# A longer ring for the expert weights, lent from the end's sum

## The chip, the cores and the metric

The kernel runs on one core of a Trainium2 chip. The metric is the time of one execution on the device, in microseconds (us); for the kernel before it is the median of three runs. One more execution was recorded by the hardware profiler, and all rows below are from it.

## The reference

One layer of a conditioned hybrid decoder: 1024 tokens of width 1024 (T and D below), all float32. Shift, scale and gate vectors come from a projection of a conditioning vector.

```
h   = modulate(x)                          # shift and scale of the conditioning vector
x1  = LayerNorm(alpha*x + gate * mixer(h)) # conformer convolution beside an SSD scan, one output projection
h2  = modulate(x1)
MoE : top group of 8, then the top 2 of its 8 experts (64 experts in all)
      y = (silu(h2 @ w1[e]) * (h2 @ w3[e])) @ w2[e],  w1, w3: 1024x512, w2: 512x1024
      f = sum over the token's 2 experts of gate_prob * y
out = LayerNorm(alpha*x1 + gate2 * f)      # ln2_g, ln2_b
```

Each expert has 3 matrices of 2 MB. All 64 experts are 384 MB, and the kernel reads nearly all of it once.

## The kernel before

The program has three stages, one after the other. The first (to about 940 us) computes the adaLN projection, the input projection, the convolutions, the scan and the output projection; its last step is the output projection `mix` (L480), for which SP loads the weights `wo` (L927). It ends with a router for each 128 tokens, and it leaves the normalised rows x1 without their scale and shift in DRAM, in `td`. The second (to about 955 us) builds tables: which token stands in which place of which expert, as one-hot comparisons `rows` (L1214 to L1221) that are multiplied on TensorE, with the index columns `gidx` and `ridx` as the result. The third is the mixture of experts, and then the second LayerNorm, here called the end.

The third stage does 32 units, in a fixed order by a string of letters (ORDER). A unit gathers 128 rows of `td` by `gidx` (L1294, POOL), transposes them (`tp`, L1302), and multiplies: h0 and h1 (L1332) with w1 and w3, a product and a transpose (`s1`, `hT`, L1337 to L1344), and yp (L1351) with w2. VectorE scales the result to y (L1356), and POOL scatters it to `ybuf` by `ridx` (L1288). A unit is made of one expert with 128 rows (H), two experts with 64 (F and L) or four with 32 (S); a T is a pair of experts with three units, `t`, `t..x` and `t`, where the middle one uses both. So S takes 24 weight tiles of 1 MB, L and F take 12, H takes 6, and T takes 12 for three units. In names such as `h0t4x` or `yps` the letters after h0, h1 or yp are the kind of unit. The last unit is an S; 18 of its 24 tiles are loaded only on a condition, that an expert has rows, which does not hold for these inputs.

The weight tiles (`load`, L238 to L243, [128, 2048] float32) come on SP's queue in the order of use. `plan` numbers all 384 of them, and the ring has N_RING = 14 slots: tile n goes to `ring[n % 14]`, and is asked for when the last use of tile n - 14 has been emitted. Slots 0 to 7 (N_RING_A) belong to a pool that lives through the first stage; four of them (4 to 7) carry the `wo` columns before. 13 tiles (N_EARLY) are asked for before the first gather: 4 in the program step F ahead of `wo_2_5` and the later ones, and so on through `load_fixed`, whose expert numbers are known before the tables.

The end's sum needs acc = alpha*(ln1_g*td + ln1_b) for each 128 tokens. `load_sum(i)` (L1270 to L1278) does row block i: a load on ScalarE's queue (L1275), a multiply and an add on VectorE (L1276, L1277), a scaling on ScalarE (L1278). It is called after the units 4 to 11, one for each. The first call loads ln1_g and ln1_b too, into a tile with the tag yb (L1274).

The end (`finish`, L1541 to L1586) does eight row blocks. `collect` (L1280 to L1285) loads, on POOL's queue, both experts' y of each token from `ybuf`: block 0 into the tile `yb`, the other blocks into ring slots that have come free. A block's z is acc plus these two plus the last unit's own y, which is not sent through DRAM but is added by one-hot matrices (`hots` times `yhs` and `yls`, L1366 to L1373). VectorE adds one part to acc (L1556), TensorE sums the rest into PSUM (L1549 to L1560), VectorE takes the statistics (L1561, L1563), and VectorE, ScalarE and POOL normalise (L1565 to L1585). SP stores the rows (L1586). Each queue and engine works through its instructions in the order in which they were emitted; the compiler's scheduler sets that order.

The loads of the tiles wait for slots on SP's queue. Loads issued by SP and ScalarE share eight completion counters (lanes), and a new load waits until the last one of its lane has landed.

## Time and profile before

| what | value |
|---|---|
| median of three runs | 2002.7 us (2000.44 to 2003.66) |
| profiled execution: time | 2007.87 us |
| profiled execution: span, first to last instruction | 2006.1 us |
| mean granted TensorE clock | 0.959 of full speed |
| busy: PE, PEld, DVE, ACT, POOL | 89%, 50%, 48%, 28%, 25% of the span |
| bytes moved on SP's and ScalarE's queues | 551.74 MB and 42.34 MB |

PE is TensorE's matmuls, PEld its weight loads, DVE VectorE, ACT ScalarE, POOL GpSimd, SP the engine that issues most transfers. The profiled execution took 5.2 us more than the median of the runs. Busy shares are means over the three stages, which have different limits; the third stage, from about 955 us on, is to be read by itself.

### The profile page before, as it was taken

Reading aid. Unit: us, or ns where it says so; the run is one execution under the profiler, and the core shown is the slowest. Engines: PE = TensorE matmul, PEld = TensorE weight load, DVE = VectorE, ACT = ScalarE, POOL = GpSimd, SP = SyncE. Lnnn points to the kernel's source line nnn. Section 1 sums busy time; section 2 is a strip of 40 time slices with the busy share of each in tenths; the row PEclk is TensorE's granted clock in tenths of the full one; section 3 lists DMA queues with packets and bytes.
Section 4 is the critical chain, followed back from the end, with each engine's and each line's share of the span. In section 5 each row is a group of like instructions: output and inputs, shape, how many; then the busy total and the mean of one; then the engine's idle time right before and its main releaser. Section 6 shows DMA issues by size and latency. Waiting matters only on the chain.

```text
span 2006.1 us, 23809 instructions
## 1 busy us (share of the span) xinstructions
PE 1789.1 (89%) x8136; PEld 998.1 (50%) x8136; DVE 956.2 (48%) x1928; ACT 557.4 (28%) x1054; POOL 501.6 (25%) x408
## 2 busy tenths in 40 slices
PE   6899999899999999997879799788898997999786
PEld 1566667587788777886323133232242331443233
DVE  1699999869998997867113012112011110111117
ACT  0345554643555465644100011011010010111001
POOL 0457656513443465311100001000000000000014
PEclk7899999889999999998889899999999998999998
DMA  7788888656655446674899999999989999999993
GB/s 242 234 293 265 260 254 300 223 195 212 203 190 192 160 150 221 218 289 163 316 419 419 420 415 354 419 419 420 420 300 391 419 420 419 418 412 371 419 366 161
DMA packets 202328, 620.81 MB, mean 309 GB/s; under 512 B 25886, under 2 KB 91702, under 8 KB 154332
## 3 DMA queue, kind: packets, MB, share of 16 engines
q1 hardware_dynamic: 155792, 551.74, 71.8%
q10 hardware_dynamic: 36188, 42.34, 6.6%
q0 software_dynamic: 10224, 25.18, 3.3%
q8 instruction: 65, 1.06, 0.2%
q14 instruction: 59, 0.48, 0.1%
HBM read 575.07 MB, written 79.25 MB: 326 GB/s over the span
## 4 chain that ended last, share of the span: by engine, by line
PE 45%; DMA 31%; DVE 11%; issue 5%; ACT 4%; POOL 3%; ACTq 0%; SPq 0%; DVEq 0%; POOLq 0%
DMA ring<-in_expert_w_dram 25%; PE mix L480 6%; PE px L480 5%; PE h0h L1332 3%; DVE ac L605 2%; PE pg L480 2%; PE h1h L1332 2%; PE pv L480 2%; PE pz L480 2%; PE yph L1351 2%; PE yps L1351 2%; PE ypl L1351 2%; PE h1l L1332 2%; PE h0l L1332 2%; PE ypt L1351 1%
## 5 line engine op out<-in xcount | busy, mean ns | idle before, releaser
L605 DVE SCALAR_TENSOR_TENSOR ac<-u,cw,ac 128x512 f32<-128x512 f32 x394 | 295.7, 750 | 5.5
L1294 POOL DMA_INDIRECT xg<-td,gidx x32 | 32.9, 1027 | 754.8 <-PE tph L1302 206.7
L480 PE MATMUL px<-hTh,wx_hl 128*128 128x512 f32 x512 | 169.8, 401 | 1.6 <-DVE u L619 1.2
L1332 PE MATMUL h1s<-ring,xTs 128*32 128x512 f32 x512 | 105.2, 733 | 43.2 <-DMA ring<-in_expert_w_dram 43.2
L480 PE MATMUL mix<-wo_hl,cth 128*128 128x512 f32 x416 | 129.9, 405 | 1.7 <-ACT zs L726 1.1
L1351 PE MATMUL yps<-ring,hTs 128*32 128x512 f32 x512 | 109.1, 613 | 19.3 <-DMA ring<-in_expert_w_dram 16.8
L1338 DVE TENSOR_TENSOR s1s<-s1s,h1s 128x512 f32<-128x512 f32 x8 | 5.5, 688 | 220.8 <-PE h1s L1332 220.8
L480 PEld LDWEIGHTS px<-hTh,wx_hl 128*128 128x128 f32 x512 | 95.6, 188 | 30.4 <-issue 4.6
L454 POOL TENSOR_TENSOR wo_hl<-wo,wo_hl 128x512 fp32r<-128x512 f32 x52 | 74.0, 1436 | 113.3 <-ACT wo_hl L453 106.1
L480 PE MATMUL px<-hTl,wx_hl 128*128 128x512 f32 x256 | 101.3, 396 | 0.0
L480 PE MATMUL pg<-hTh,wg_hl 128*128 128x512 f32 x256 | 89.2, 419 | 2.0 <-DVE h L520 1.8
L480 PEld LDWEIGHTS mix<-wo_hl,cth 128*128 128x128 f32 x416 | 78.2, 190 | 22.0 <-DVE wo_hl L454 1.5
L1332 PE MATMUL h0s<-ring,xTs 128*32 128x512 f32 x512 | 75.4, 639 | 14.0 <-DMA ring<-in_expert_w_dram 14.0
L311 PE MATMUL ada<-wada,cond 128*32 128x512 f32 x192 | 67.7, 706 | 19.7 <-DMA wada<-in_w_ada_dram 19.7
L480 PE MATMUL pv<-hTh,wv_hl 128*128 128x512 f32 x256 | 84.0, 396 | 0.0
L480 PE MATMUL pz<-hTh,wz_hl 128*128 128x512 f32 x256 | 83.6, 397 | 0.1
L1332 PEld LDWEIGHTS h1s<-ring,xTs 128*32 128x32 f32 x512 | 22.6, 129 | 121.0 <-DMA ring<-in_expert_w_dram 76.6
L480 PE MATMUL mix<-wo_hl,ctl 128*128 128x512 f32 x208 | 77.6, 404 | 3.1 <-DVE ctl L962 3.1
L453 ACT CAST wo_hl<-wo 128x512 fp32r<-128x512 f32 x104 | 62.9, 617 | 33.0 <-PE mix L480 18.1
L1351 PEld LDWEIGHTS yps<-ring,hTs 128*32 128x32 f32 x512 | 26.7, 111 | 87.4 <-issue 46.4
L1351 PE MATMUL ypl<-ring,hTl 128*64 128x512 f32 x256 | 66.6, 598 | 2.3 <-ACT hTl L1344 2.3
L1332 PE MATMUL h0l<-ring,xTl 128*64 128x512 f32 x256 | 63.6, 598 | 3.9 <-DMA ring<-in_expert_w_dram 3.9
(622 smaller groups left out, 3465.5 us busy)
## 6 DMA issues: line engine op xcount, KB each, us to landing
ring<-in_expert_w_dram SPq DMA_DIRECT2D x384, 1024.0 KB
wo<-in_w_out_dram SPq DMA_DIRECT2D x112, 256.0 KB
wada<-in_w_ada_dram SPq DMA_DIRECT2D x96, 256.0 KB
wind<-wx_hl SPq DMA_DIRECT2D x32, 512.0 KB
wx_hl<-wind SPq DMA_DIRECT2D x32, 512.0 KB
wind<-wg_hl SPq DMA_DIRECT2D x16, 512.0 KB
wind<-wv_hl SPq DMA_DIRECT2D x16, 512.0 KB
wx<-in_w_in_dram SPq DMA_DIRECT2D x32, 256.0 KB
```

The costliest lines, as they stand in the source:

```text
L311: nc.tensor.matmul(pm[32 * j:32 * j + 32, :], lhs, wt, start=(k == 0), stop=(k == KT - 1), tile_position=(0, 32 * j))
L453: nc.scalar.copy(hi, wt)
L454: (eng or nc.gpsimd).tensor_tensor(lo, wt, hi, op=OP.subtract)
L480: nc.tensor.matmul(pt, lhs[a_], rhs[b_], start=(first and n == 0), stop=(last and n == 2))
L605: nc.vector.scalar_tensor_tensor(to, v_, w_, run_, op0=OP.mult, op1=OP.add)
L1294: nc.gpsimd.indirect_dma_start(out=t_, out_offset=None, in_=td, in_offset=bass.IndirectOffsetOnAxis(ap=gcol, axis=0), bounds_check=T - 1, ...
L1332: nc.tensor.matmul(hp[a:b, :], xT[:, 4 * hf + k, a:b], w_[:, k, :], start=(hf + k == 0), stop=(hf + k == 4), tile_position=(0, a))
L1338: nc.vector.tensor_tensor(s1, s1, hps[1], op=OP.mult)
L1351: nc.tensor.matmul(yps[n][a:b, :], hT[:, 2 * hf + k, a:b], w_[:, k, 512 * n:512 * n + 512], start=(hf + k == 0), stop=(hf + k == 2), tile_ ...
```

## The change

The ring gets 20 slots. Ten belong to the pool that lives from the first stage on, four to the second pool, and six are lent: a new tile `lent`, the four quarters of `acc`, and one tile `lend`. Up to tile 339 all 20 slots are used in turn; for the last 44 tiles (N_BACK) only the 14 own ones, by the lists `slot` and `before`. 16 tiles are asked for ahead of the first gather.

As acc now holds weights, `load_sum` is called for all eight blocks after the unit with index len(units) - 3, the first of the last two L units. ln1_g and ln1_b are loaded into `lent`, which later takes block 0 of `ybuf`. The one-hot table `rows` has a tile of its own, and the last unit's hots and its y's high half lie in the tile with the tag `lend`.

```diff
@@ -30,9 +30,11 @@
 EPS = 1e-5
 BIG = 1.0e30
 OOB = float(1 << 20)
-N_RING = 14
-N_RING_A = 8
-N_EARLY = 13
+N_RING = 20
+N_RING_A = 10
+N_EARLY = 16
+N_LEND = 6
+N_BACK = 44
@@ -1146,6 +1148,7 @@
     toff = rt2.tile([P, 8], F32, name="toff")
     nc.gpsimd.iota(toff, pattern=[[P, 8]], base=0, channel_multiplier=0, allow_small_or_imprecise_dtypes=True)
     acc = rt2.tile([P, 8, D], F32, name="acc")
+    lent = rt2.tile([P, 2048], F32, name="lent")
     gidx = rt2.tile([P, NU_STAT], I32, name="gidx")
     ridx = rt2.tile([P, NU_STAT], I32, name="ridx")
     ridx_o = rt2.tile([P, NU_OVF], I32, name="ridx_o")
@@ -1176,7 +1179,8 @@
         def t2(nm, shape, dt=F32):
             return wk.tile(shape, dt, name=nm)
         V = nc.vector
-        ring += [ringb.tile([P, 2048], F32, name=f"ring{j}") for j in range(N_RING_A, N_RING)]
+        ring += [ringb.tile([P, 2048], F32, name=f"ring{j}") for j in range(N_RING_A, N_RING - N_LEND)]
+        ring += [lent] + [acc[:, 2 * j:2 * j + 2, :].rearrange("p a d -> p (a d)") for j in range(4)] + [None]
         load_fixed(ring, N_RING_A, N_EARLY, fix_i)
@@ -1211,7 +1215,7 @@
         V.scalar_tensor_tensor(u_, over, 4096.0, u_, op0=OP.mult, op1=OP.add)
         V.tensor_tensor(r_, r_, pos, op=OP.add)
         b16 = lambda t_: t_[:, :, None].to_broadcast([P, 16, NU_STAT])
-        rows = acc[:, 0, :].bitcast(BF16).rearrange("p (j t) -> p j t", t=P)
+        rows = t2("rows", [P, 16, P], BF16)
         hot = t2("hot", [P, 16, NU_STAT], BF16)
         V.tensor_tensor(hot, jf[:, None, 0:NU_STAT].to_broadcast([P, 16, NU_STAT]), b16(u_), op=OP.is_equal)
         hv = t2("hv", [P, 2, 16, NU_STAT], BF16)
@@ -1260,6 +1264,7 @@
         bufs_of = {"z": ZPB, "h0": 1, "h1": 1, "tp": TPB, "yp": 2}
         g2_bc = wk.tile([P, D], F32, bufs=1, name="g2_bc")
+        ring[N_RING - 1] = wk.tile([P, 2048], F32, tag="lend", bufs=1, name="lend")
         uno = [0]
         half = [slice(512 * n, 512 * n + 512) for n in range(2)]
@@ -1268,8 +1273,7 @@
         def load_sum(i):
             if i == 0:
-                l1_ = wk.tile([P, 2, D], F32, tag="yb", bufs=1, name="l1")
-                l1[:] = [l1_[:, 0], l1_[:, 1]]
+                l1[:] = [lent[:, 0:D], lent[:, D:2 * D]]
                 for t_, v_ in zip(l1, (ln1_g, ln1_b)):
                     tc.keep_in_program_order(nc.scalar.dma_start(t_, bc(v_, 0, D)))
             tc.keep_in_program_order(nc.scalar.dma_start(acc[:, i, :], td[i * P:(i + 1) * P, :]))
@@ -1280,7 +1284,7 @@
         def collect():
             for i in range(8):
-                yy = wk.tile([P, 2, D], F32, tag="yb", bufs=1, name="yb") if i == 0 else spare[i].rearrange("p (k d) -> p k d", k=2)
+                yy = (spare[i] if i else lent).rearrange("p (k d) -> p k d", k=2)
                 nc.gpsimd.dma_start(yy, ybuf[2 * i * P:2 * (i + 1) * P, :].rearrange("(t k) d -> t k d", k=2))
                 yield yy
@@ -1362,13 +1366,15 @@
             nc.vector.tensor_scalar(trel, toff, -1.0, tcol, op0=OP.mult, op1=OP.add)
             hots = []
             for j in range(0, 8, HW):
-                hot = wk.tile([P, HW, P], F32R, tag="hot", bufs=1, name=f"hot{nm}_{j}")
+                held = wk.tile([P, 2048], F32R, tag="lend", bufs=1, name="held")
+                hot = held[:, 0:HW * P].rearrange("p (j t) -> p j t", t=P)
                 nc.vector.tensor_tensor(hot, jf[:, None, :].to_broadcast([P, HW, P]),
                                         trel[:, j:j + HW, None].to_broadcast([P, HW, P]), op=OP.is_equal)
                 hots += [hot[:, i, :] for i in range(HW)]
             ys = []
+            yls = wk.tile([P, D], F32R, tag="xT", bufs=BF[0], name=f"yl{nm}")
             for n in range(2):
-                yh, yl = (wk.tile([P, 512], F32R, tag=f"y{p_}", bufs=2, name=f"y{p_}{nm}_{n}") for p_ in "hl")
+                yh, yl = held[:, D + 512 * n:D + 512 * n + 512], yls[:, half[n]]
                 nc.scalar.copy(yh, y[:, half[n]])
                 nc.vector.tensor_tensor(yl, y[:, half[n]], yh, op=OP.subtract)
                 ys.append((yh, yl))
@@ -1472,11 +1478,11 @@
             while sent[0] < len(plan):
                 n = sent[0]
-                if n >= N_RING and uses[n - N_RING] > 0:
+                if before[n] is not None and uses[before[n]] > 0:
                     break
                 r, which, hf = plan[n]
                 if n >= min(N_RING, 6 * N_FIX):
-                    load(ring[n % N_RING], *place_regs(r), which, hf)
+                    load(ring[slot[n]], *place_regs(r), which, hf)
                 sent[0] += 1
         def need(rs, times):
@@ -1493,7 +1499,7 @@
                 n = where[r, which, hf]
                 assert n < sent[0]
                 uses[n] -= 1
-                return ring[n % N_RING]
+                return ring[slot[n]]
             return of
         units = []
@@ -1525,16 +1531,26 @@
             add(kind, first[kind])
             first[kind] += step[kind]
         assert list(first.values()) == [P_TRI, P_HVY, P_LGT, P_SML, NE]
+        slot, before = [], []
+        turn = [(s_, None) for s_ in range(N_RING)]
+        for n in range(len(plan)):
+            while n >= len(plan) - N_BACK and turn[0][0] >= N_RING - N_LEND:
+                turn.pop(0)
+            s_, b_ = turn.pop(0)
+            slot.append(s_)
+            before.append(b_)
+            turn.append((s_, n))
         emitted()
         for n, (nm, places, u) in enumerate(units[:-1]):
             if n == 3:
                 overflow_tables()
             unit(nm, [tiles(r) for r in places], cols_of(u))
-            if 4 <= n < 12:
-                load_sum(n - 4)
-
-
-        spare = [ring[(len(plan) + j) % N_RING] for j in range(N_RING)]
+            if n == len(units) - 3:
+                for i in range(8):
+                    load_sum(i)
+
+
+        spare = [ring[s_] for s_, _ in turn]
         l2g_bc, l2b_bc = spare[0][:, 0:D], spare[0][:, D:2 * D]
         banks = [("z", "z"), ("h0", "h1"), ("tp", "tp"), ("yp", "yp")] * 2
```

The compiled order of the instructions shows what moves. Line numbers of the changed kernel are four to sixteen higher.

ScalarE in the kernel before, from its last product `s1s` to the end's first operations; the eight loads of acc stand far ahead of this, between the units 4 and 12:

```order
L1344 COPY hTl_12411<-thl_12406 128x512
L1309 ACTIVATE xTs_12444<-tps_0_12445,modc 128x128 x4
L1337 ACTIVATE s1s_12539<-h0s_12463 128x512
L1590 DMA ring_8112<-in_ln_g_dram 128x1024
L1591 DMA ring_8112<-in_ln_b_dram 128x1024
L1344 COPY hTs_12547<-ths_12542 128x512
L1372 CAST yhs_0_12590<-ys_12583 128x512
L1372 CAST yhs_1_12594<-ys_12583 128x512
L1565 ACT_TABLE_LOAD
```

ScalarE now, from the last unit's `s1s` to the load of the fifth row block (acc<-td is the load of a row block, acc<-acc the scaling of the one before, held the high half of the last unit's y):

```order
L1341 ACTIVATE s1s_12547<-h0s_12471 128x512
L1282 ACTIVATE acc<-acc 128x1024
L1279 DMA acc<-td 128x1024
L1606 DMA ring_6721<-in_ln_g_dram 128x1024
L1607 DMA ring_6721<-in_ln_b_dram 128x1024
L1348 COPY hTs_12555<-ths_12550 128x512
L1282 ACTIVATE acc<-acc 128x1024
L1279 DMA acc<-td 128x1024
L1378 CAST held<-ys_12591 128x512 x2
L1282 ACTIVATE acc<-acc 128x1024
L1279 DMA acc<-td 128x1024
```

These are the loads of the third, fourth and fifth row block. Ahead of these rows the load of the first stands behind the hT of unit 29, with two loads into lent before it, and the load of the second behind the last unit's `xT` copies. Behind these rows the pair of a scaling and a load comes three times more, then the last scaling and the ACT_TABLE_LOAD. So each load stands behind the scaling of the row block before, and four of the eight are behind the casts of the last unit's y.

VectorE in the kernel before, from the last unit's y (ys) on (BN_STATS are the statistics of the second LayerNorm, the adds with yb and ring those of the rows from `ybuf`):

```order
L1356 SCALAR_TENSOR_TENSOR ys_12583<-yps_0_12549,gslot,g_bc 128x512
L1556 TENSOR_TENSOR acc<-acc,yb 128x1024
L1373 TENSOR_TENSOR yls_0_12591<-ys_12583,yhs_0_12590 128x512
L1356 SCALAR_TENSOR_TENSOR ys_12583<-yps_1_12550,gslot,g_bc 128x512
L1556 TENSOR_TENSOR acc<-acc,ring_8133 128x1024
L1373 TENSOR_TENSOR yls_1_12595<-ys_12583,yhs_1_12594 128x512
L1561 BN_STATS bs_12621<-z_0_12609 128x6
L1556 TENSOR_TENSOR acc<-acc,ring_8648 128x1024
L1561 BN_STATS bs_12644<-z_0_12613 128x6
L1556 TENSOR_TENSOR acc<-acc,ring_8649 128x1024
```

VectorE now, from the seventh block's add of its rows from `ybuf` on (L1280 and L1281 are the multiply and the add of the eighth block with ln1_g and ln1_b, in lent):

```order
L1572 TENSOR_TENSOR acc<-acc,ring_8116 128x1024
L1280 TENSOR_TENSOR acc<-acc,lent 128x1024
L1281 TENSOR_TENSOR acc<-acc,lent 128x1024
L1572 TENSOR_TENSOR acc<-acc,ring_8137 128x1024
L1572 TENSOR_TENSOR acc<-acc,lent 128x1024
L1577 BN_STATS bs_12625<-z_0_12613 128x6
L1577 BN_STATS bs_12648<-z_0_12617 128x6
L1577 BN_STATS bs_12648<-z_1_12618 128x6
L1577 BN_STATS bs_12671<-z_0_12621 128x6
L1577 BN_STATS bs_12671<-z_1_12622 128x6
```

The statistics, which stood between the adds, now stand behind the last of the eight adds, and that last one is the add of block 0 from lent. The transfers that feed the adds are POOL's:

```order
L1288 DMA ring_6722<-ybuf 128x2048
L1288 DMA ring_6723<-ybuf 128x2048
L1288 DMA ring_6724<-ybuf 128x2048
L1288 DMA ring_8074<-ybuf 128x2048
L1288 DMA ring_8095<-ybuf 128x2048
L1288 DMA ring_8116<-ybuf 128x2048
L1288 DMA ring_8137<-ybuf 128x2048
L1288 DMA lent<-ybuf 128x2048
L1600 TENSOR_TENSOR lent<-lent,ring_6721 128x512
```

The load of block 0 into lent was the first of eight and is now the last; it takes the place of ln1_g and ln1_b, so it is behind the last operation of VectorE that reads them.

## Rows read from the trace of the kernel before

**Rows 1.** The view of busy time by stretches of 20 us over the third stage. The columns are the stretch in us, its length, the busy us of PE, PEld, DVE, ACT and POOL with the number of instructions, the granted TensorE clock as a share of full speed, the mean busy share of the DMA engines, and what they moved in GB/s.
```profile
940.00:960.00 20.00, 9.26 (x73) 8.12 (x73) 13.69 (x57) 2.28 (x4) 2.26 (x2) 0.50 0.14 41
960.00:980.00 20.00, 18.88 (x82) 6.78 (x82) 2.06 (x5) 5.17 (x11) 0.99 (x1) 0.89 0.71 270
980.00:1000.00 20.00, 20.00 (x96) 7.55 (x92) 2.78 (x6) 0.81 (x2) 2.02 (x2) 1.00 1.02 418
...
1180.00:1200.00 20.00, 19.15 (x85) 8.56 (x83) 4.51 (x8) 1.76 (x4) 2.03 (x2) 1.00 1.01 413
1200.00:1220.00 20.00, 19.71 (x66) 8.10 (x66) 6.27 (x10) 2.91 (x6) 2.96 (x2) 1.00 0.82 313
1220.00:1240.00 20.00, 18.86 (x72) 7.91 (x72) 5.82 (x9) 3.54 (x7) 3.07 (x2) 1.00 0.94 363
...
1460.00:1480.00 20.00, 18.86 (x91) 8.11 (x92) 2.62 (x6) 2.59 (x6) 2.04 (x2) 1.00 0.85 317
1480.00:1500.00 20.00, 19.15 (x62) 8.46 (x58) 3.46 (x7) 0.87 (x2) 2.04 (x2) 1.00 0.66 224
1500.00:1520.00 20.00, 19.71 (x79) 7.69 (x80) 2.78 (x6) 2.32 (x6) 2.03 (x2) 1.00 0.95 353
1520.00:1540.00 20.00, 18.60 (x122) 6.32 (x118) 3.46 (x7) 2.59 (x6) 2.03 (x2) 1.00 1.01 412
...
1800.00:1820.00 20.00, 18.86 (x55) 8.99 (x54) 3.37 (x7) 1.60 (x4) 2.04 (x2) 1.00 0.94 367
1820.00:1840.00 20.00, 19.66 (x120) 6.49 (x118) 2.87 (x6) 1.59 (x4) 2.03 (x2) 1.00 0.88 337
...
1980.00:2000.00 20.00, 10.87 (x30) 5.32 (x29) 15.21 (x29) 4.29 (x8) 14.06 (x10) 0.88 0.42 172
```

**Rows 2.** The chain that ended last, in order of time, around one of the pairs that make three units (start us, us, what); the chain is the piece of work, or of a transfer, that the next one waited for.
```profile
1144.49 26.09 DMA ring<-in_expert_w_dram
...
1176.65 7.13 PE ypt L1351 x16
...
1200.49 7.09 PE ypt4x L1351 x32
```

**Rows 3.** The waits of SP's queue from 850 us on (what was waited for: us in total, times, longest).
```profile
SPq L243 <- DMA ring<-in_expert_w_dram: 503.5, 254, 11.5
...
SPq L243 <- PE h0t L1332: 22.6, 5, 8.0
...
SPq L243 <- PE h0t6x L1332: 17.0, 2, 13.2
```

**Rows 4.** SP's timeline around the early weight tiles (start us, us, queue, line, operation, out<-in, count).
```profile
869.95 16.01 SPq L243 DMA_DIRECT2D ring<-in_expert_w_dram  x8
891.08 21.24 SPq L927 DMA_DIRECT2D wo<-in_w_out_dram  x14
```

**Rows 5.** VectorE's timeline in the routing step (start us, us, engine, line, operation, out<-in, shape), two of its small operations.
```profile
941.60 0.16 DVE L1237 TENSOR_TENSOR rest<-gate_all,gp 128x16 f32<-128x16 f32 x1
...
945.07 0.42 DVE L900 TENSOR_REDUCE pos_all<-r_po 128x4 f32<-128x256 f32 x1
```

**Rows 6.** ScalarE's timeline at the start of the loads for the end's sum (columns as in rows 5).
```profile
1153.16 0.34 ACTq L1274 DMA_DIRECT2D l<-in_ln_g_dram  x1
1155.65 0.34 ACTq L1274 DMA_DIRECT2D l<-in_ln_b_dram  x1
```

**Rows 7.** The view of one tile, td, the matrix of token rows in DRAM: its direct loads into acc (duration of the issue in ns, minimum, median and maximum, and the first and last start in us), and the time to landing of the transfers that name it.
```profile
L1275 ACTq DMA_DIRECT2D acc<-td x8: 326/327/353, 1158.8 to 1351.7; - x8
...
DMA to landing us min/median/max: 3.7/8.4/10.0
```

**Rows 8.** The view by lines, from 960 to 1950 us: the three operations on a loaded row of acc (busy us, mean ns | idle before, releaser).
```profile
L1277 DVE TENSOR_TENSOR acc<-acc,l 128x1024 f32<-128x1024 f32 x8 | 9.8, 1223 | 0.2
L1276 DVE TENSOR_TENSOR acc<-acc,l 128x1024 f32<-128x1024 f32 x8 | 9.7, 1218 | 1.5 <-DMA acc<-td 1.5
...
L1278 ACT ACTIVATE acc<-acc 128x1024 f32<-128x1024 f32 x8 | 8.4, 1054 | 29.8 <-DVE acc L1277 19.4 <-DMA ring<-in_expert_w_dram 10.4
```

**Rows 9.** The DMA issues from 1930 us to the end (KB each, median us from issue to landing).
```profile
ring<-ybuf POOLq DMA_DIRECT2D x7, 1024.0 KB, 11.6
...
yb<-ybuf POOLq DMA_DIRECT2D x1, 1024.0 KB, 7.7
```

**Rows 10.** VectorE's timeline at the end of the program (columns as in rows 5).
```profile
1955.00 0.75 DVE L1356 SCALAR_TENSOR_TENSOR ys<-yps,gslot,g_bc 128x512 f32<-128x512 f32 x1 [9.53 <-PE yps L1351]
...
1959.80 0.69 DVE L1561 BATCH_NORM_STATS2 bs<-z 128x6 f32<-128x512 f32 x1
...
1993.76 1.77 DVE L1582 SCALAR_TENSOR_TENSOR ring<-ring,rs,ring 128x1024 f32<-128x1024 f32 x1
```

**Rows 11.** The view by lines of VectorE from 1955 to 1996 us: the adds of the sum.
```profile
L1556 DVE TENSOR_TENSOR acc<-acc,ring 128x1024 f32<-128x1024 f32 x7 | 9.3, 1330 | 0.0
```

**Rows 12.** TensorE's timeline in one of the last rows of the sum (columns as in rows 5).
```profile
1982.00 1.02 PE L1549 MATMUL z<-ring,ident 128*128 128x512 f32 x2
1982.46 0.79 PE L1559 MATMUL z<-yhs,hots 128*128 128x512 f32 x1
1983.09 0.40 PE L1559 MATMUL z<-yls,hots 128*128 128x512 f32 x1
1983.32 1.02 PE L1560 MATMUL z<-acc,ident 128*128 128x512 f32 x2
```

## Prediction

> **What bounds the kernel now.** I read the stretches of the third stage first. The reader is to look at the GB/s column [rows 1]: in most stretches the transfers move 418 to 420 GB/s, at a busy share of 1.0 (the stretch from 980 to 1000) [rows 1], so a tile of 1 MB (1.0486 million bytes) costs 2.50 us, and the stage is bound by the weight stream. What can be won there is the time in which the stream stands: the start (940 to 980), two places around the T units (1180 to 1240, 1460 to 1540), and 1800 to 1840. The chain [rows 2] shows the same: it is a weight transfer up to 1170 us and TensorE's own matmuls in the T units that follow. The waits of SP's queue tell which release is late there. Most of the queue's waiting, 503.5 us, is for the stream itself; but a wait for a matmul such as h0t (22.6 us) or h0t6x (17.0 us) is one for a slot [rows 3]. A T needs 12 tiles, thus 30 us of stream, while its three units keep TensorE busy for 72 us (three times some 24 us, the distance from one ypt to ypt4x in the chain). The ring fills, and the stream stops.
>
> Then I read the end. It starts with the last unit's y, which VectorE takes at 1955.0, and VectorE's last operation is done at 1995.5 [rows 10]: 40.5 us in which VectorE hardly rests. The rest up to the span's end, 10.6 us, I leave as it is.
>
> **What the change gives, before the last unit's y.** Losses are against 419 GB/s: 20 us times the missing share.
>
> *Start.* Two stretches lose 18.0 us (41 GB/s) and 7.1 us (270 GB/s) [rows 1]. Three tiles more ahead of the gather use 7.5 us of the first, and four tiles behind it, where one was, fill the 7.1 us of the second. That is 14.6 us. Against it: the order puts some eight small VectorE operations of 0.16 us behind the reduction that gives pos_all [rows 5], on the path to the gather's index, 1.2 us. And SP now asks for ten tiles, not eight, ahead of the next `wo` columns, 5.0 us more stream. Between the eighth tile and the next `wo` load SP now stands from 885.96 to 891.08 [rows 4], 5.1 us, so the two fit in the gap; I charge 2 us of the possible 5 to the projection. Start: 14.6 - 1.2 - 2 = about 11 us (8 to 13).
>
> *First pair place, 1180 to 1240* (413, 313 and 363 GB/s): 0.3 + 5.1 + 2.7 = 8.0 us [rows 1]. Six slots more are 15 us of stream ahead, which covers it: 8 us (5 to 8).
>
> *Second, 1460 to 1540* (317, 224, 353, 412): 4.9 + 9.3 + 3.2 + 0.3 = 17.7 us [rows 1]. The six slots cover 15 of it: 15 us (9 to 17.7).
>
> *1800 to 1840* (367 and 337): 2.5 + 3.9 = 6.4 us [rows 1], covered: 6.4 us (3 to 6.4). The last 44 tiles have 14 slots again, as before.
>
> *Moved bytes.* The eight loads of acc, 0.5 MB each, leave the stretch 1158.8 to 1351.7 [rows 7], and ln1's 1 MB goes with them: 12.5 us of stream. About a third of that stretch is the first pair place, where they cost nothing, so 8.4 us go; ln1 and perhaps three rows come back ahead of the last y, partly where the stream is about to end. I take 4 us (0 to 8.4).
>
> *ScalarE's queue near the end.* Three loads now stand there ahead of the transposes' copies of the next unit. When such loads were issued before, they came at 1153.16 and 1155.65 [rows 6], one tile's time apart: each waited for a weight tile in its lane. I charge 2 us (0 to 5).
>
> Together 11 + 8 + 15 + 6.4 + 4 - 2 = **42.4 us** earlier at the last y (bounds, term by term, 20 to 54; the low ends all together are unlikely).
>
> **What it costs, behind the last y.** Let Y be the start of VectorE's first operation on that y. The order shows four loads of acc behind the casts of y, each behind the scaling of the row block before it. So the cover that hid them, units 4 to 11, is gone, and each link of the chain is a load, a multiply, an add and a scaling. A load's own landing was not shown; the transfers naming td, gathers of the same 512 KB, took 3.7 us at the least and 8.4 us in the median, under the full stream [rows 7]. Once the weights have ended the load is nearest to the least, so I take 3.7. With 1.22, 1.22 and 1.05 us [rows 8] and 0.4 us for hand-overs a link is 7.6 us. The fifth row's load is issued at about Y + 5, behind the two casts and the fourth row's scaling. The eighth row's add is done at Y + 5 + 3 x 7.6 + 3.7 + 2.4 + 0.4 = Y + 34.3. The Trainium skill, page "DMA: Bandwidth & Descriptors", section "Anatomy of one DMA", gives 2.0 us plus the bytes at 436 GB/s, an estimated 3.2 us for such a load; by it the chain would be 2 us shorter. No row here shows a load that short.
>
> Only then may block 0 of `ybuf` be loaded into lent. Its like took 7.7 us alone and 11.6 us beside others [rows 9]; I take the first, as nothing else moves: Y + 42. The add of 1.3 us [rows 11] ends at Y + 43.3. All statistics now stand behind that add. Before, 1959.8 to 1995.5, 35.7 us, held six of the adds, 8.0 us [rows 10, 11], so 27.7 us of VectorE are left: the end is at Y + 71.0, not Y + 40.5. That is **30.5 us** later (bounds: 24.4 with a link of 7.0 and a reload of 4.0; 49 with every load at 8.4). Moving the hots comparison and the new places of the y halves cost nothing: they lie in units in which VectorE waits for TensorE.
>
> **Sum.** -42.4 + 30.5 = -11.9 us. Against the profiled execution that is 2007.9 - 11.9 = 1996.0. It lies 5.2 us above the median of the runs, a difference that is in no term, so against the median I forecast 2002.7 - 11.9 = **1990.8 us**, faster.
>
> **Rivals.**
>
> *A: more is won.* All stalls go and the tail's chain is short: 13 + 8 + 17.7 + 6.4 + 8.4 = 53.5 us won, 24.4 lost: 1973.6. For it: the stream is at its rate wherever slots are free. Against it: the last pair place is longer than six slots, and ScalarE's loads wait in lanes. Chance 0.17.
>
> *B: TensorE's clock.* In the chain of loads TensorE has next to nothing to do, and its granted clock was 0.50, the level of 1.2 GHz, in the routing step where it was busy for 9.3 of 20 us, and 0.88 in the last rows of the end [rows 1]. A row block's z takes 1.02 + 0.79 + 0.40 + 1.02 = 3.2 us of TensorE there [rows 12], about VectorE's own pace. At half the clock four blocks take 4 x 3.2 = 12.8 us more, and the sum is +0.9: 2003.6, no change. Against it: the clock came back within 20 us at the stage's start, to 0.89 and 1.00 [rows 1]. The Trainium skill, page "TensorE: Matmul & The Clock Gate", section "What's actually happening", says that an idle array falls to half its clock and that activity brings it back; by that rule this rival's first rows of z would be slow and the later ones not. The trace agrees with the fall. Chance 0.13.
>
> *C: slower, by the chain of loads alone.* The seven loads of `ybuf` rows, 1 MB each, are under way around Y too. If each of the four loads takes 8.4 us, not 3.7, the tail loses 4 x 4.7 = 18.8 us more, and the time is 2002.7 - 11.9 + 18.8 = 2009.6. It decides from a load of 3.7 + 11.9/4 = 6.7 us on. For it: the median of rows 7. Against it: `ybuf` is some 17 us of transfers, and the chain is longer. Chance 0.13.
>
> *D: the ring does not fill.* If it is TensorE's order of releases and not the number of slots that stops the stream, the three stalls stay: 11 + 4 - 2 = 13 us won, 30.5 lost, 2020.2. Against it are the waits for h0t and h0t6x, which are waits for slots [rows 3]. Chance 0.07.
>
> **How the numbers follow.** My forecast has 0.50. A measurement of this kernel tells 0.2% (4 us) from no change. Faster: 0.50 + 0.17 = 0.67; the same: B, 0.13; slower: C and D, 0.20. The range from 1974 to 2009 reaches from A's figure to C's and leaves out D and about half of what A and C have beyond their figures. Cases of one sign hold most of the chance; the forecast's own range is 1984 to 1997.
>
> **What would show it.** In the changed profile the stretches around the T units hold 400 GB/s or more, and SP's waits for h0t and h0t6x shrink; the stream starts about 11 us earlier; the last y is at about 1955.0 - 42 = 1913. Behind it VectorE idles for DMA acc<-td four times, 3 to 5 us each; the first statistics come about 43 us after y, and the last operation some 71 us after it. I am wrong if the last y is not at least 32 us earlier, if statistics come less than 35 us behind it, or if TensorE is what VectorE waits for in the last four row blocks.

## The result and the profile after

The changed kernel takes 2022.2 us (median of five runs, 2013.9 to 2022.5) against 2002.7 us: the ratio is 1.009, with a 95% interval of 1.0069 to 1.011. It is slower, by some 18 us by the ratio (19.5 us between the medians); forecast was 1990.8 us and faster. The profiled execution has a span of 2020.4 us, 14.3 us more than before, and it splits in two at the last unit's y. That y starts at 1930.1 us, not 1955.0: 24.9 us won, where 42.4 were forecast. From there to VectorE's last operation it takes 78.1 us, not 40.5: 37.6 us lost, where 30.5 were forecast. Behind that operation the rest is 12.1 us, not 10.6.

The stretches of the third stage that answer to [rows 1], with the same columns:

```profile
940.00:960.00 20.00, 9.04 (x71) 7.85 (x71) 12.66 (x58) 2.27 (x3) 2.26 (x2) 0.50 0.40 143
960.00:980.00 20.00, 18.88 (x86) 7.34 (x86) 2.05 (x5) 5.11 (x11) 0.99 (x1) 0.90 0.94 380
...
1200.00:1220.00 20.00, 18.86 (x56) 8.71 (x56) 1.70 (x5) 2.59 (x6) 0.78 (x1) 1.00 0.96 390
1220.00:1240.00 20.00, 18.86 (x92) 7.46 (x90) 2.36 (x5) 2.59 (x6) 1.26 (x2) 1.00 0.99 402
...
1440.00:1460.00 20.00, 18.86 (x59) 8.44 (x56) 2.05 (x5) 2.59 (x6) 2.04 (x2) 1.00 0.84 349
1460.00:1480.00 20.00, 18.55 (x89) 7.64 (x89) 4.88 (x9) 2.09 (x5) 3.01 (x3) 1.00 0.43 141
1480.00:1500.00 20.00, 18.86 (x70) 7.39 (x68) 2.19 (x3) 2.59 (x6) 0.98 (x1) 1.00 1.01 402
...
1780.00:1800.00 20.00, 16.86 (x72) 4.98 (x68) 2.65 (x4) 1.18 (x2) 2.01 (x2) 0.92 0.94 369
1800.00:1820.00 20.00, 17.72 (x86) 6.41 (x78) 1.69 (x5) 1.99 (x5) 0.76 (x1) 0.91 0.78 306
```

The start and the first pair place (1200 to 1240) came out near the forecast: 143 and 380 GB/s instead of 41 and 270, and 390 and 402 instead of 313 and 363. The second place did not. It now lies at 1440 to 1500, and with 349, 141 and 402 GB/s it loses 3.3 + 13.3 + 0.8 = 17.4 us, as much as before (17.7). From 1780 to 1820 the stream loses 2.4 + 5.4 = 7.8 us, more than the 6.4 before. What SP waited for in the second place, the answer to [rows 3] from 1430 to 1500 us:

```profile
SPq L245 <- PE ypt6x L1355: 30.0, 2, 27.8
```

One wait of 27.8 us, for a matmul that multiplies with w2. TensorE's timeline tells why:

```profile
1429.70 7.13 PE L1355 MATMUL ypt<-ring,hTt 128*128 128x512 f32 x16
1436.76 7.08 PE L1336 MATMUL h1t6x<-ring,xTt6x 128*64 128x512 f32 x30
...
1446.72 1.02 PE L1336 MATMUL h0t<-ring,xTt 128*128 128x512 f32 x2
...
1463.26 1.08 PE L1336 MATMUL h0l<-ring,xTl 128*64 128x512 f32 x4 [0.60 <-ACT xTl L1313]
...
1469.70 7.02 PE L1355 MATMUL ypt6x<-ring,hTt6x 128*64 128x512 f32 x30
```

Unit t6x (two experts of a pair) has its last h1 done at 1443.8. Its ypt6x, which would give its w2 tiles back, starts only at 1469.7, behind the whole h0 and h1 of the next unit and behind a part of h0l and h1l of the one after it. ypt of the unit before stands in the middle of t6x too. In the kernel before, a unit's yp came ahead of the next unit's h0 throughout, but for two matmuls at 1820.3 us. The compiled order of TensorE had changed with the ring. The forecast rests on the new orders of ScalarE, VectorE and GpSimd, and on TensorE's order of before.

Near the end ScalarE's queue held a unit up. Its rows, and TensorE's wait for it:

```profile
1870.41 0.34 ACTq L1278 DMA_DIRECT2D lent<-in_ln_g_dram  x1
1872.91 0.34 ACTq L1278 DMA_DIRECT2D lent<-in_ln_b_dram  x1
1876.05 0.33 ACTq L1279 DMA_DIRECT2D acc<-td  x1
1876.50 1.51 ACT L1313 ACTIVATE xTl<-tpl,modc 128x128 f32<-128x128 f32 x4 [18.21 <-DMA ring<-in_expert_w_dram]
```

```profile
PE h0l L1336 <- ACT xTl L1313: 7.0, 1, 7.0
```

The three loads stood ahead of the copies xTl of unit 30, each waiting for a weight tile, as in [rows 6]. ScalarE stood idle for 18.2 us ahead of those copies, of which TensorE lost 7.0; 2 were charged.

VectorE behind the last y, which answers to [rows 10]:

```profile
1930.09 0.75 DVE L1360 SCALAR_TENSOR_TENSOR ys<-yps,gslot,g_bc 128x512 f32<-128x512 f32 x1 [5.44 <-PE yps L1355]
...
1945.19 1.23 DVE L1280 TENSOR_TENSOR acc<-acc,lent 128x1024 f32<-128x1024 f32 x1 [4.87 <-DMA acc<-td]
...
1951.21 1.23 DVE L1280 TENSOR_TENSOR acc<-acc,lent 128x1024 f32<-128x1024 f32 x1 [1.18 <-DMA acc<-td]
...
1957.15 1.23 DVE L1280 TENSOR_TENSOR acc<-acc,lent 128x1024 f32<-128x1024 f32 x1 [1.11 <-DMA acc<-td]
...
1963.33 1.23 DVE L1280 TENSOR_TENSOR acc<-acc,lent 128x1024 f32<-128x1024 f32 x1 [1.35 <-DMA acc<-td]
...
1971.23 1.23 DVE L1572 TENSOR_TENSOR acc<-acc,lent 128x1024 f32<-128x1024 f32 x1 [3.07 <-DMA lent<-ybuf]
1976.51 4.88 DVE L1577 BATCH_NORM_STATS2 bs<-z 128x6 f32<-128x512 f32 x8 [4.05 <-PE z L1576]
...
1991.95 0.70 DVE L1577 BATCH_NORM_STATS2 bs<-z 128x6 f32<-128x512 f32 x1 [0.99 <-PE z L1576]
...
2006.47 1.76 DVE L1598 SCALAR_TENSOR_TENSOR ring<-ring,rs,ring 128x1024 f32<-128x1024 f32 x1
```

The four links of the chain are seen as the rows L1280 that wait for DMA acc<-td. The first came 15.1 us behind y, the others 6.0, 5.9 and 6.2 us behind one another. VectorE idled 4.87 us for the first and 1.1 to 1.4 us for the others, not 3 to 5 us each. The add of block 0 begins at 1971.2, and the first statistics at 1976.5, 46.4 us behind y (43 were forecast): they wait for TensorE's z. TensorE there:

```profile
1971.25 3.44 PE L1565 MATMUL z<-lent,ident 128*128 128x512 f32 x4 [19.79 <-DMA lent<-ybuf]
...
1975.45 1.88 PE L1576 MATMUL z<-acc,ident 128*128 128x512 f32 x4
1982.52 2.07 PE L1565 MATMUL z<-ring,ident 128*128 128x512 f32 x2 [5.19 <-DVE lent L1590]
...
1989.58 1.02 PE L1565 MATMUL z<-ring,ident 128*128 128x512 f32 x2
```

Four matmuls of 512 columns take 3.44 us, where the same number takes 1.88 us further down, and a pair takes 2.07 instead of 1.02. The granted clock, in the column ahead of the last two, is 0.50, the level of 1.2 GHz, in the chain of loads, and again low from 1981 to 1988; from 1988 to 2004 it is 1.00:

```profile
1954.00:1974.00 20.00, 2.75 (x4) 1.21 (x5) 9.80 (x8) 4.17 (x4) 0.53 (x1) 0.50 0.29 105
...
1981.00:1988.00 7.00, 5.48 (x9) 2.71 (x9) 6.97 (x20) 3.05 (x7) 2.36 (x2) 0.51 0.00 0
```

The reload of block 0 took 5.1 us, less than the 7.7 of [rows 9], which was not a load alone but the first of eight:

```profile
lent<-ybuf POOLq DMA_DIRECT2D x1, 1024.0 KB, 5.1
```

### The profile page after: what moved, and what is told of

It reads as the page before. It is cut to its first block, busy times and chain, and to the rows that moved or that the text cites. A ratio compares the mean times of both kernels' runs of the same rounds, so it can differ in the third digit from the quotient of the medians.

```text
span 2020.4 us, 23739 instructions
## 1 busy us (share of the span) xinstructions
PE 1785.5 (88%) x8136; PEld 995.2 (49%) x8136; DVE 952.5 (47%) x1928; ACT 557.4 (28%) x1054; POOL 497.1 (25%) x408
## 3 DMA queue, kind: packets, MB, share of 16 engines
q8 instruction: 65, 1.06, 0.2%
## 5 line engine op out<-in xcount | busy, mean ns | idle before, releaser
L1355 PE MATMUL yps<-ring,hTs 128*32 128x512 f32 x400 | 85.0, 612 | 13.8 <-DMA ring<-in_expert_w_dram 9.8
L1336 PE MATMUL h1s<-ring,xTs 128*32 128x512 f32 x368 | 72.2, 709 | 17.9 <-DMA ring<-in_expert_w_dram 17.9
L1342 DVE TENSOR_TENSOR s1h<-s1h,h1h 128x512 f32<-128x512 f32 x8 | 5.5, 688 | 142.9 <-PE h1h L1336 142.9
L482 PEld LDWEIGHTS pg<-hTh,wg_hl 128*128 128x128 f32 x256 | 50.9, 200 | 22.8 <-issue 4.7
L747 POOL TENSOR_TENSOR dec<-ab,future 128x512 f32<-128x512 f32 x32 | 43.0, 1343 | 74.2 <-DMA ab<-acsd 44.0
L1336 PE MATMUL h0s<-ring,xTs 128*32 128x512 f32 x368 | 54.2, 603 | 7.2 <-DMA ring<-in_expert_w_dram 6.4
L749 ACT ACTIVATE dec<-dec,nacs 128x128 f32<-128x128 f32 x128 | 41.1, 391 | 56.7 <-POOL dec L747 56.5
```

Of the source, the lines that this page charges most:

```text
L482: nc.tensor.matmul(pt, lhs[a_], rhs[b_], start=(first and n == 0), stop=(last and n == 2))
L747: nc.gpsimd.tensor_tensor(dec, ab, future[:, None, :].to_broadcast([P, 4, P]), op=OP.add)
L749: nc.scalar.activation(dec[:, r, :], dec[:, r, :], AF.Exp, bias=acs[:, cl, 4 * g + r:4 * g + r + 1])
L1336: nc.tensor.matmul(hp[a:b, :], xT[:, 4 * hf + k, a:b], w_[:, k, :], start=(hf + k == 0), stop=(hf + k == 4), tile_position=(0, a))
L1342: nc.vector.tensor_tensor(s1, s1, hps[1], op=OP.mult)
L1355: nc.tensor.matmul(yps[n][a:b, :], hT[:, 2 * hf + k, a:b], w_[:, k, 512 * n:512 * n + 512], start=(hf + k == 0), stop=(hf + k == 2), tile_ ...
```

## The experiments

A run of one kernel is not like the next in its first stage: the first gather came at 947.9 to 963.1 us in the eleven profiles used here. So where the mechanism is in the third stage I compare two times within a profile: from the first unit's y to the last one's (A), and from there to VectorE's last operation (the tail). Before, A is 970.7 us and the tail 40.5; with the change 945.8 and 78.1. Each ratio is to runs of the kernel before on the same chip. The kernel pinned and unchained ran twice: A and the tail are of the second run, the ratio is of the first.

| kernel | A, us | tail, us | ratio to before, with interval |
|---|---|---|---|
| before | 970.7 | 40.5 | 1 |
| the change | 945.8 | 78.1 | 1.009 (1.0069 to 1.011) |
| order pinned | 934.0 | 79.9 | 1.0017 (0.9998 to 1.0036) |
| order pinned, kernel before | 968.3 | 40.5 | one run |
| tail alone | 970.7 | 77.4 | 1.0195 (1.0155 to 1.0235) |
| block 0 later | 945.7 | 71.7 | 1.0071 (1.005 to 1.0093) |
| loads unchained | 949.8 | 46.3 | 0.9943 (0.9921 to 0.9965) |
| pinned and unchained | 948.2 | 47.1 | 0.9911 (0.9876 to 0.9945) |
| sum one unit earlier | 949.0 | 40.2 | 0.990 (0.988 to 0.992) |
| sum in the gap | 943.2 | 40.4 | 0.9876 (0.9854 to 0.9899) |
| 15 slots, acc kept | 962.8 | 41.7 | 0.9993 (0.9974 to 1.0012) |

**The order of the units on TensorE, pinned.** In `unit`:

```diff
+                            if hf + k == 0 and nm != "ov":
+                                behind(m_, tail)      # first h0, h1 matmuls: issued after the last unit's yp
...
+                            if hf + k == 2:
+                                ends.append(m_)       # last yp matmuls
...
+            tail[:] = ends
```

> The changed kernel with one rule more: the first h0 matmuls of a unit stand behind the yp matmuls of the unit before on TensorE. Theory 1 (the compiled order put yp of some units, ypt6x above all, behind later units' h0 and h1, so that their w2 tiles stay in the ring): the stretches 1440 to 1500 lose at most 5 us against 419 GB/s, not 17.4; the last y comes at about 1917, not 1930.1; the tail stays at some 78 us; the time is about 2009. Rival (the lead of a ring is a stock that the first pair already used up, and TensorE is the limit in the second): the stall stays near 17 us, the last y within 3 us of 1930, the time about 2022.

A fell by 11.8 us against the change, and the second place lost 3.0 + 4.8 = 7.8 us, not 17.4:

```profile
1440.00:1460.00 20.00, 16.74 (x76) 7.13 (x75) 3.37 (x7) 2.59 (x6) 2.03 (x2) 0.92 1.01 419
1460.00:1480.00 20.00, 19.44 (x58) 7.64 (x54) 1.86 (x3) 0.60 (x1) 1.98 (x2) 0.99 0.93 356
1480.00:1500.00 20.00, 19.43 (x78) 8.20 (x80) 3.01 (x7) 2.59 (x6) 2.05 (x2) 1.00 0.88 318
```

```profile
1456.72 8.78 PE L1366 MATMUL ypt6x<-ring,hTt6x 128*64 128x512 f32 x32 [2.12 <-DVE yt L1374]
1465.44 7.13 PE L1344 MATMUL h0t<-ring,xTt 128*128 128x512 f32 x16
```

ypt6x now starts at 1456.7, ahead of the next unit's h0. The first theory holds, with some more left of the stall (7.8 us, not 5). The last y was at 1926.3 rather than 1917, since this run's first stage was 8 us late. What is left of the stall goes with TensorE's own pace: from 1410 to 1520 it never waited longer than 2.1 us, while SP's queue waited there 10.6 us for ypt6x, 8.1 for ypt and 8.0 for h0l. The tail is nearly unchanged, and the whole, 2010.8 us (about 2009 forecast), is level with the kernel before (2006.9 on that chip).

**The same rule in the kernel before**, as a control:

> A control: the kernel before with the units' order on TensorE pinned by the same rule. Theory (its compiled order already goes unit by unit): from the first unit's y to the last one's it takes 970 us, as without the rule, within 3 us. Rival (the rule itself makes something faster or slower, so that the gain with the change says nothing on the ring): more than 5 us away from that.

A is 968.3 us in its one run, 2.4 us below the kernel before and inside the 3 us. So the rule alone brings next to nothing; it gives the longer ring back what the new order had taken.

**The tail alone.** The kernel before, and only this moved:

```diff
-            if 4 <= n < 12:
-                load_sum(n - 4)
+            if n == len(units) - 3:
+                for i in range(8):
+                    load_sum(i)
```

> The kernel before (14 slots, acc its own) with nothing changed but the place of the eight acc loads: behind unit 29, as in the change. Theory 1 (the chain of loads behind the last y is the whole cost of the tail): the last y comes up to 8 us earlier than 1955.0, as the loads leave the middle, and is held some us by ScalarE's queue; from it to VectorE's last operation it takes about 78 us, not 40.5; the time is about 2036. Rival (the tail's cost comes from the lent tile and its late block 0, and from the ring): the tail takes at most 65 us and the time is below 2026.

```profile
1947.74 0.75 DVE L1356 SCALAR_TENSOR_TENSOR ys<-yps,gslot,g_bc 128x512 f32<-128x512 f32 x1 [4.95 <-PE yps L1351]
...
1993.43 4.88 DVE L1562 BATCH_NORM_STATS2 bs<-z 128x6 f32<-128x512 f32 x8 [4.11 <-PE z L1561]
...
2023.43 1.76 DVE L1583 SCALAR_TENSOR_TENSOR ring<-ring,rs,ring 128x1024 f32<-128x1024 f32 x1
```

From y at 1947.7 to the end of the last operation at 2025.2 it is 77.4 us, with 14 slots and nothing lent. The ratio of 1.0195 is 39 us; the median, 2043.4, is above the 2036 forecast. So the place of the loads is the whole of the tail's loss, and neither the ring nor the new tile adds to it. The late block 0 is a part of that: here too its load came last, as the tile yb holds ln1's two vectors until the eighth row is done, and its add came at 1988.1. A did not change. Counted from the first y, the stream was 6.2 us ahead of the kernel before up to tile 351, and 1.4 us behind it at tile 372: of the ten loads that left the middle six come back ahead of the last y, and they hold ScalarE's queue up there (TensorE waited 11.1 us for xTl of unit 30 in this run).

**Block 0 later.** The change with `for i in [1, 2, 3, 0, 4, 5, 6, 7]` in `finish`, for the order in which the blocks' z is begun as well.

> The changed kernel with the end's row blocks written in the order 1, 2, 3, 0, 4 to 7, so that the scheduler places the statistics of blocks 1 to 3 ahead of the wait for block 0. Theory (statistics behind all adds are a part of the tail of 78.1 us, some 27 us of VectorE's work that could lie in the chain's idle time): three of eight blocks' statistics and products, some 10 us, go into the chain of loads; the tail is 68 us, the time about 2012. Rival (the end is set by TensorE's or GpSimd's work behind block 0, or by the clock): the tail stays above 74 us.

The tail fell to 71.7 us, between theory (68) and rival (74), but the stores behind VectorE's last operation now end 16.4 us after it, not 12.1, so that 2 us are won in all. The ratio is 1.0071 against 1.009, with intervals that overlap. Where the statistics stand is a small part of the loss; the chain ahead of them is the large one.

**The loads unchained.** The change, with all ten loads on GpSimd's queue ahead of the first multiply:

```diff
                 for t_, v_ in zip(l1, (ln1_g, ln1_b)):
-                    tc.keep_in_program_order(nc.scalar.dma_start(t_, bc(v_, 0, D)))
-            tc.keep_in_program_order(nc.scalar.dma_start(acc[:, i, :], td[i * P:(i + 1) * P, :]))
+                    tc.keep_in_program_order(nc.gpsimd.dma_start(t_, bc(v_, 0, D)))
+                for j in range(8):
+                    tc.keep_in_program_order(nc.gpsimd.dma_start(acc[:, j, :], td[j * P:(j + 1) * P, :]))
```

> The changed kernel with the ten loads of the end's sum issued on GpSimd's queue, all eight of acc ahead of the first multiply, so that no load stands behind a scaling. Theory 1: ScalarE no longer waits 7 us in its queue at unit 30, so the last y comes at about 1923; the tail is 41 to 46 us, as before the change; the time is about 1980. Rival (the loads run into the row loads from ybuf and the late statistics are TensorE's clock, not the chain): the tail is still 55 us or more, the time 1993 or more.

The tail fell from 78.1 to 46.3 us, and the time to 0.9943 of before, 1994.5 us. I had expected 1980: A rose to 949.8, though TensorE no longer waited for xTl. VectorE and TensorE show where that went:

```profile
1913.38 1.22 DVE L1281 TENSOR_TENSOR acc<-acc,lent 128x1024 f32<-128x1024 f32 x1
...
1932.53 0.75 DVE L1361 SCALAR_TENSOR_TENSOR ys<-yps,gslot,g_bc 128x512 f32<-128x512 f32 x1
...
1977.53 1.28 DVE L1599 SCALAR_TENSOR_TENSOR ring<-ring,rs,ring 128x1024 f32<-128x1024 f32 x1
```

```profile
1914.99 7.13 PE L1356 MATMUL yps<-ring,hTs 128*32 128x512 f32 x64 [0.73 <-ACT hTs L1349]
```

TensorE was done with yps at 1922.1. VectorE took it at 1932.5: sixteen operations on acc, from 1913.4 on, stood ahead of it in its queue as one block of 19 us, though VectorE had been idle before.

**Pinned and unchained together**, in a first run:

> Both edits on the changed kernel: the units' order on TensorE pinned and the ten loads unchained on GpSimd's queue. Theory 1: the two add up: last y at about 1910, tail 41 to 46 us, time about 1967, some 36 us below the kernel before. Rival (order costs nothing): as with the loads unchained alone, about 1980.

and in a second, whose profile is used here:

> The same kernel as with both edits, pinned order and unchained loads, for an undisturbed profile. Theory: from the first y to the last 937 to 945 us (the pinned order's 934, with the block of sixteen VectorE operations ahead of the last y), tail 41 to 46 us. Rival (the block costs its whole 19 us): 950 us or more.

The first run gave 1989.0 us, a ratio of 0.9911, above both forecasts (1967 and 1980). In the second A is 948.2, between the two forecasts: yps ended at 1925.7, and the same block held y until 1936.2, 10.5 us.

**The sum one unit earlier.** Both edits, `N_BACK = 72`, and `load_sum` behind the unit with index len(units) - 4.

> The changed kernel with the units' order pinned, the ten loads unchained on GpSimd's queue, and the sum taken one unit earlier: the loads behind unit 28 and the last 72 tiles, not 44, on the 14 own slots. Theory: with the loads unchained, the sixteen VectorE operations on acc stood as one block of 19 us ahead of the last y, which was ready 10.4 us earlier; one unit earlier they lie in the 25 us in which VectorE waits for unit 30. From the first unit's y to the last one's it takes about 935 us, the tail 41 to 46 us, and the time is about 1970. Rival (the shorter ring for the last 72 tiles costs what this gives, or the block holds unit 30's product up): from first to last y 945 us or more, the time 1982 or more.

The tail was 40.2 us, that of the kernel before. A stayed at 949.0 and the time at 1984.2, as the rival said, because the shorter ring from tile 312 on cost what the block had cost. The block, from 1876.1 to 1895.4, no longer held a y or unit 30's s1 up. From 1740 to 1820 the stream lost 1.5 + 8.8 + 5.1 + 1.4 = 16.8 us:

```profile
1740.00:1760.00 20.00, 19.15 (x57) 7.58 (x54) 1.91 (x2) 0.60 (x1) 0.00 (x0) 1.00 0.98 388
1760.00:1780.00 20.00, 17.59 (x42) 8.28 (x43) 4.09 (x8) 1.99 (x5) 3.01 (x3) 0.83 0.64 235
1780.00:1800.00 20.00, 18.86 (x67) 8.48 (x69) 3.47 (x7) 2.59 (x6) 2.42 (x3) 1.00 0.85 313
1800.00:1820.00 20.00, 17.42 (x134) 6.02 (x127) 1.22 (x3) 2.59 (x6) 0.89 (x2) 1.00 0.98 389
```

**The sum in the gap.** As the run before, with `N_BACK = 48`, and the sixteen operations ahead of unit 30's s1 by a rule like that of the first experiment.

> As the sum taken one unit earlier (order pinned, loads on GpSimd's queue behind unit 28), but with the last 48 tiles on the own slots, not 72, and the sixteen VectorE operations on acc ahead of unit 30's product s1 by a rule. Theory: the stalls of 1740 to 1800, some 17 us, came from the shorter ring; with them gone it takes about 936 us from the first unit's y to the last one's, the tail stays at 40 to 42 us, the time is about 1972. Rival (the block of 19 us holds unit 30's product up, or the stalls stay): 945 us or more, time 1981 or more.

```profile
1760.00:1780.00 20.00, 17.59 (x49) 8.36 (x49) 2.68 (x6) 2.59 (x6) 3.01 (x3) 1.00 1.01 411
1780.00:1800.00 20.00, 18.86 (x92) 7.90 (x94) 3.37 (x7) 2.00 (x5) 2.03 (x2) 1.00 0.99 396
```

```profile
1868.68 1.22 DVE L1282 TENSOR_TENSOR acc<-acc,lent 128x1024 f32<-128x1024 f32 x1
...
1886.70 1.23 DVE L1283 TENSOR_TENSOR acc<-acc,lent 128x1024 f32<-128x1024 f32 x1
1891.98 0.69 DVE L1354 TENSOR_TENSOR s1l<-s1l,h1l 128x512 f32<-128x512 f32 x1 [4.05 <-PE h1l L1346]
...
1927.96 0.75 DVE L1378 SCALAR_TENSOR_TENSOR ys<-yps,gslot,g_bc 128x512 f32<-128x512 f32 x1 [9.56 <-PE yps L1370]
```

The stalls went (411 and 396 GB/s where 235 and 313 were). The block lay from 1868.7 to 1887.9, and unit 30's s1 at 1891.98 waited for TensorE behind it, not for the block. As the block had cost nothing in the run before either, the gain is that of the longer ring, not of the rule. A came to 943.2, not 936. What is missing is the loads' own bytes: counted from the first y, the stream's lead on the kernel before fell from 39.6 us at tile 340 to 27.1 at tile 351, the 12.5 us that ten loads of 0.5 MB take, and A is 27.5 us below that of the kernel before. This is the fastest of all kernels here: 1980.9 us, ratio 0.9876 (0.9854 to 0.9899), 24 us below the 2005.1 of the kernel before on the same chip.

**15 slots, acc kept.** The change with `N_RING = 15`, `N_EARLY = 14`, `N_LEND = 1` (the tile lend), and `load_sum` behind the units 4 to 11 again.

> The changed kernel without what it lends from the end: 15 slots (14 and lend), 14 tiles ahead of the gather, acc its own and loaded behind the units 4 to 11 as before. Theory (the start's gain comes from the four tiles behind the gather and the few ahead of it, the pair places' gain from slots): the stream starts about 9 us earlier than before, the pair places give 2 to 5 us, the tail is as before, 41 to 45 us; the time is about 1990. Rival (the early tiles hold up the projection or the routing step by as much): within 4 us of the kernel before.

A fell by 7.9 us, and the tail is as before, but the median is 2002.9 against 2004.8, with a ratio of 0.9993, as the rival said. Counted from the first y, the stream was ahead by 2.4 us at tile 28, not 9, so the start's gain of the change needs its slots; at the pair places and behind them the lead grew to 6.5 at tile 280. The profile shows this gain and the times don't bear it out; with the first stage scattering by 15 us, what it is worth stays open.

## Why the prediction was wrong

The two main terms were the right ones, and of the right sign. The gain was put too high and the cost too low, and the sum of -11.9 us came out as +14.3 against the profiled execution.

*What held.* The stream was ahead by 12.7 us from the start (11 forecast; read as the landing of the same tiles in the two traces): 7.5 us by the three early tiles and 5.2 in the stretch from 960 to 980, where 7.1 were forecast. The gather was 0.8 us later (1.2 forecast), but between profiles it varies by more. The first pair place gave 8.0 - 2.2 = 5.8 us (8). The moved bytes gave more than forecast in the middle: tile 168, behind the last of the moved loads, landed 31.5 us earlier than before, and 31.5 - 12.7 - 5.8 is 13.0, about the whole of the 12.5 us, not 4. That is a remainder, and it depends on the slots: with 14 slots (the tail alone) the lead grew by 6.8 us between tiles 78 and 168. It was also lent and not won. The lead was 31.9 at tile 351 and 28.4 at tile 357, behind the first three loads that come back. The eighth row's add was done at Y + 35.7, forecast Y + 34.3, though by other parts: the first load took 8.8 us (issued at 1936.4, among the row loads), and the links behind it 6.0 us, not 7.6. That these two errors cancel is luck. The load of block 0 ended earlier than forecast, its add at Y + 42.4 (Y + 43.3).

*The step that failed: "The six slots cover 15 of it"*, for the second pair place, and with it "covered" for 1800 to 1840. They gave 0 and -1.4 us. I took the order of TensorE's work, and so the moment at which a slot comes free, from the trace before. The change had moved it: yp of several units went behind the next unit's products. Counted from the first y, ypt6x started at 485.4 us, and at 464.4 with the order pinned: the slots that the change added were held 21 us longer, and that is no slot won. With the order pinned 9.6 us of the 17.4 came back, and A fell by 11.8. Rival D gave 2020.2 us, near to what was measured. It named the order of releases, which is what held at the second place, but it had all three stalls stay, and the first went; and its tail was 7.1 us too short. That its number is so near is in part luck.

*ScalarE's queue*: 2 us were taken from a range of 0 to 5, and TensorE lost 7.0 (9.7 with the order pinned, 11.1 with the tail alone, none with the loads on GpSimd's queue). The row showed the queue moving at the pace of one tile per load; three loads at that pace are 7.5 us, and I should have multiplied.

*The tail*: 37.6 us, not 30.5. The chain came out at its size. What came behind it was not: from the add of block 0 to VectorE's last operation it took 35.8 us, not 27.7. VectorE waited 4.05 us for TensorE's first z and three times more for later ones (0.99, 1.48 and 1.48), 8.0 us in all, the whole difference. So TensorE's work on z, put at nothing behind the chain, was a term of the sum. Rival B had the place right and only a part of the reason. Block 0's z took TensorE 6.1 us, the first 3 of them at the lower clock, where an earlier block's had taken 4.5 (1946.9 to 1951.5), and the first two halves of the next z took 4.4 and 2.6 us, where later ones took 2.2: an estimate of 4.3 us, at most, for the clock, not 12.8. The rest came at full clock. Half a z is 2.2 us of TensorE and 0.70 of VectorE's statistics, and with all adds done VectorE had nothing to put between them; TensorE itself had stood for 5.2 us until VectorE had read the first z (L1590). That TensorE stands for 20 us ahead of these matmuls followed from my own chain. The Trainium skill, page "TensorE: Matmul & The Clock Gate", section "What's actually happening", has an idle array fall to half its clock and activity bring it back; the rows agree (3.44 us for four matmuls at first, 1.88 further down).

In the sum, the gain was 17.5 us short, the tail 7.1 too short and the end 1.6: 26.2 us, which is the difference between -11.9 and +14.3. Of the prediction's three signs of being wrong two came: the last y was 24.9 us earlier, not 32 or more, and VectorE waited for TensorE three times in the last four row blocks.

The change's idea was worth having. With the order kept, the loads off ScalarE's queue and the sum in VectorE's idle time, the same 20 slots (14 for the last 48 tiles) give 1.2% instead of costing 0.9%.

## What to carry to other kernels

Where a scheduler sets the order, read the new order of the engine that *releases* the resource, and not only of those that wait: a buffer's gain is counted from when it comes free. Work that was hidden because it lay among other work should be priced as a chain when it is moved to the end: count what each load stands behind in its queue, and look for a queue with nothing else to do, and for idle time with a place in the order. And bytes moved out of one stretch of a full stream come back in another: here 12.5 us. A step that leaves TensorE idle by your own estimate takes its lower clock, and its pace where no other work covers it, into the sum.

## What was not expected of the hardware

The first stage, the same work but for up to three more early tiles, ended at times that differ by 15 us between profiles: the first gather came at 947.9 us in one and 963.1 us in another. Differences below some 8 us were therefore read within a profile, from the first unit's y.

The links of the chain took 6.0 us, not 7.6, because a load that stands behind a scaling in ScalarE's queue goes out as the scaling starts, not as it ends. ScalarE's timeline of the changed kernel, one link:

```profile
1947.71 1.06 ACT L1282 ACTIVATE acc<-acc 128x1024 f32<-128x1024 f32 x1 [10.30 <-DVE acc L1281]
1947.72 0.33 ACTq L1279 DMA_DIRECT2D acc<-td  x1
```

The scaling starts at 1947.71 and the load is issued at 1947.72; its row's multiply starts at 1951.21, so the load took 3.5 us. The link is 3.5 us and the 2.5 of VectorE's two operations, without the 1.06 of the scaling. The Trainium skill's 2.0 us plus the bytes at 436 GB/s (page "DMA: Bandwidth & Descriptors", section "Anatomy of one DMA", where it is given for transfers that GpSimd issues), an estimate of 3.2 us, is near that; this load stands on ScalarE's queue.
